# Mixer A's last three row tiles turned by VectorE and DRAM, 1/sum moved into the gate stage, PSUM banks and work order assigned anew

## The chip, the cores and the metric

One core of one Trainium2 chip. The metric is the device time of one execution in microseconds; of the kernel before it is the median of three runs. Instructions run on five engines, each in its own order: TensorE (PE; its weight loads are listed as PEld), VectorE (DVE), ScalarE (ACT), GpSimd (POOL) and SyncE (SP), whose queue issues every DMA of this kernel.

## The reference

One layer of a streaming encoder for a prompt group (1024 rows) and a sample group (32 rows), width 1024, two kinds of attention with 8 heads of 64 each, all in float32:

```python
hn = rmsnorm(h, g_pre)
qa, ka, va, ga, qb, kb, vb, gb = split(hn @ w_in)          # 8 blocks of 512 columns
# A: softmax over the row's own 64-row chunk and the 8 before it, with a clipped relative bias
s = qa @ ka.T * 64 ** -0.5 + bias_table[:, clip(k_pos - q_pos, -128, 128) + 128]
oa = softmax(where(ok, s, -1e30)) @ va
# B: stick breaking, strictly causal
z = qb @ kb.T * 64 ** -0.5
log_1m = where(causal, log_sigmoid(-z), 0)
after = cumsum(log_1m, reverse=True) - log_1m
ob = where(causal, exp(log_sigmoid(z) + after), 0) @ vb
y = concat(oa * silu(ga), ob * silu(gb)) @ w_out
h = h + rmsnorm(y, g_post)
h = h + sigmoid(h @ w_ple_gate) * (p @ w_ple)
```

The outputs are h of both groups and the new keys and values. The sample group attends to cached keys and values beside its own 32.

## The kernel before

**Precision.** Each float32 operand is split into a high part (float32r) and the remainder. A product is then two or three float32r matmuls that accumulate in one PSUM bank. The names ending in `h` and `l`, as `wTh` and `wTl`, are these parts.

**Stages.** First the rows are normalized and turned (`norm_tile`, `turn_x`), while the part `p @ w_ple` of the first four row tiles is computed (`Ple`). Then come eight pairs of heads, in the order A0, B0, A1, B1, A2, B2, A3, B3. While a pair's attention runs, `weave` lays the projections of the next pair (`col_steps`: 24 matmuls of 352 columns for each of 3 column chunks) between its steps. Beside the last pair the eight gate blocks are projected (`gA`, `gB`). Then follow the output projection and the gate of the layer input, each as a block product with seven multiplications for each 2x2 of blocks, whose combined weight blocks (`sum_weights`) are prepared during the attention stages and kept in DRAM.

**Attention of one head** (`attention`). Rows are taken in eight tiles `i` of 128. An A tile reads `cost(i)` key blocks of 128: 1, 2, 3, 4 and then 5 for each of tiles 4 to 7. `scores` multiplies into `S` banks. For A a VectorE operation adds the bias into `w0` (`om`) and keeps the extremum in `m` (`stat`); ScalarE takes the exponential into `w1` (`be`) with the row's sum; VectorE takes the reciprocal of the sum and GpSimd scales `w1` by it. For B there are two sigmoids, a running product on VectorE and a product on GpSimd.

`weights_t` turns the weights, so that keys lie on partitions. On the common path TensorE transposes each 128x128 block into a `T` bank (`ptw`), ScalarE copies up to four blocks to the high part (`wTh`) and VectorE subtracts for the low part (`wTl`). Tiles named in `ROUND` (A: tile 5; B: tiles 4, 5, 6) go another way: VectorE turns 32x32 squares from `w1` to `w0`, one DMA writes them to a DRAM tensor `swap`, four DMAs read them back with the squares in their turned places into `w1`, and the same two engines split the result from there. `values` multiplies the turned weights with V into one `PV` bank for each half of the rows, and the sum of its two halves (`ot`) goes to DRAM (`o_dr`).

**Gates.** A gate chunk (`col_steps`, kind `g`) loads its part of `o_dr` (`og`), takes the sigmoid of its product on ScalarE, multiplies by the product on VectorE and by `og` on GpSimd, and stores to `og_dr`.

**Space.** PSUM has eight banks, shared out by kind: two for projections (`mm`), three for scores (`S`), two for transposes (`T`), one for values (`PV`), each kind taken in turn. In SBUF `w0` and `w1` come out of two rings, `ring0` (`om`, 3076 columns) and `ring1` (`be`, 3640 columns); the other tiles have a tag with a fixed number of buffers.

**Order.** Every operation is recorded with what it must follow. `order` simulates the engines with costs for each operation and emits, whenever an engine is free, the ready operation with the smallest key. The key is a class, then the place in the recording plus a shift from the tables `AHEAD_OF` (by engine and tile name) and `AHEAD_AT` (by stage too). For TensorE the class puts attention (0) ahead of projections (1). All instructions are emitted from line 515, so the profile tells them apart by tile names alone.

Of the kernel before, what the change touches and what calls it, by code (L numbers as in the profile page):

```python
# [28 lines left out]
    ('ACT', 'L'): 329, ('ACT', 'S'): -1196, ('ACT', 'be'): -16, ('ACT', 'kd'): 796,  # L29
    ('ACT', 'newh'): -56, ('ACT', 'oT'): -600, ('ACT', 'om'): -36, ('ACT', 'p'): -23,  # L30
    ('ACT', 'v'): 51, ('DVE', 'Kl'): 1140, ('DVE', 'Vh'): -16, ('DVE', 'gT'): -158,
    ('DVE', 'om'): -178, ('DVE', 'ot'): 166, ('DVE', 'uu'): -34, ('DVE', 'vt'): 131,
    ('DVE', 'wl'): 758, ('DVE', 'wls'): 131, ('POOL', 'kl'): 934, ('POOL', 'wl'): 27,
    ('SP', 'GP'): 272, ('SP', 'Kcs'): -461, ('SP', 'be'): 17, ('SP', 'o'): 49,
    ('SP', 'pp'): -611, ('SP', 'stv'): -823,
}
AHEAD_AT = {
    (0, 'ACT', 'sq'): -249, (0, 'DVE', 'pleo'): -309, (1, 'ACT', 'stv'): 1111, (1, 'DVE', 'stat'): -309,
    (1, 'PE', 'ptw'): 174, (2, 'ACT', 'be'): 54, (2, 'ACT', 'v'): 127, (2, 'ACT', 'wTh'): -885,
    (2, 'ACT', 'wh'): -57, (2, 'DVE', 'S'): -238, (2, 'DVE', 'ot'): -112, (2, 'DVE', 'vx'): -293,  # L40
    (3, 'ACT', 'Kh'): -162, (3, 'ACT', 'be'): 443, (3, 'ACT', 'ot'): -574, (3, 'ACT', 'stq'): 399,
    (3, 'ACT', 'w'): 692, (3, 'ACT', 'wTh'): -1352, (3, 'DVE', 'Kcs'): -84, (3, 'DVE', 'S'): -1167,
    (3, 'DVE', 'Vh'): 222, (3, 'DVE', 'w'): -332, (3, 'PE', 'PV'): 1076, (3, 'PE', 'Ss'): 1432,
    (3, 'SP', 'kd'): -118, (3, 'SP', 'kl'): -63, (4, 'ACT', 'be'): 76, (4, 'ACT', 'om'): 38,
    (4, 'DVE', 'S'): -1067, (4, 'DVE', 'vt'): -1007, (4, 'DVE', 'wTl'): 571, (5, 'ACT', 'stq'): -509,
    (5, 'ACT', 'wh'): 1431, (5, 'DVE', 'stat'): 886, (5, 'DVE', 'vt'): -279, (5, 'POOL', 'om'): -449,
    (6, 'ACT', 'be'): 27, (6, 'ACT', 'v'): 29, (6, 'ACT', 'wTh'): 103, (6, 'DVE', 'om'): 123,
    (6, 'DVE', 'ot'): 37, (6, 'POOL', 'ksS'): 600, (6, 'POOL', 'om'): 364, (6, 'SP', 'be'): 463,
    (7, 'ACT', 'newh'): 1036, (7, 'ACT', 'wTh'): -428, (7, 'DVE', 'L'): -198, (7, 'DVE', 'S'): 1202,
    (7, 'DVE', 'Vl'): -1133, (7, 'DVE', 'kt'): 76, (7, 'DVE', 'om'): 204, (7, 'DVE', 'w'): -825,  # L50
    (7, 'DVE', 'wTl'): -310, (7, 'PE', 'ptw'): 1440, (7, 'SP', 'bias'): -214, (7, 'SP', 'o'): 69,
    (7, 'SP', 'swap'): -328, (8, 'ACT', 'sgg'): -941, (8, 'DVE', 'S'): -79, (8, 'DVE', 'Vl'): 272,
    (8, 'DVE', 'om'): 183, (8, 'DVE', 'sgg'): -911, (8, 'POOL', 'sgg'): 256, (8, 'SP', 'Kcs'): 610,
# [4 lines left out]
}  # L58
# [14 lines left out]

def f(ap):

    return ap.bitcast(F32)

# [443 lines left out]
def stream_step(  # L521
# [945 lines left out]
    for k in range(2):  # L1467
        ple.load_w(k, 0)
# [516 lines left out]
```

## Time and profile before

| | us |
|---|---|
| median of 3 runs (lowest, highest) | 776.47 (776.36, 776.52) |
| the profiled execution | 776.69 |
| its span, first to last instruction | 774.8 |

One profiled execution is read throughout. Rows of grouped instructions give the engine, the operation, the tile written and the tiles read (numbers left out), the shape and the count, then busy time and the mean in ns of one instruction, then the engine's idle time ahead of them with what ended it. Rows in order of time start with the start and the time covered, in us from the span's start. Rows of one tile's instructions give the least, the median and the largest duration in ns, and the first and last start. Rows of DMAs give the count, the KB of each and the median us from issue to landing.

### The profile page before, as it was taken

Reading aid. Unit: us, or ns where it says so; the run is one execution under the profiler, and the core shown is the slowest. Engines: PE = TensorE matmul, PEld = TensorE weight load, DVE = VectorE, ACT = ScalarE, POOL = GpSimd, SP = SyncE. Lnnn points to the kernel's source line nnn. Section 1 sums busy time; section 2 is a strip of 40 time slices with the busy share of each in tenths; the row PEclk is TensorE's granted clock in tenths of the full one; section 3 lists DMA queues with packets and bytes.
Section 4 is the critical chain, followed back from the end, with each engine's and each line's share of the span. In section 5 each row is a group of like instructions: output and inputs, shape, how many; then the busy total and the mean of one; then the engine's idle time right before and its main releaser. Section 6 shows DMA issues by size and latency. Waiting matters only on the chain.

```text
span 774.8 us, 14446 instructions
## 1 busy us (share of the span) xinstructions
PE 764.6 (99%) x4486; PEld 706.7 (91%) x4486; DVE 600.0 (77%) x1127; ACT 526.7 (68%) x1138; POOL 473.1 (61%) x551
## 2 busy tenths in 40 slices
PE   8999999999999999999999999999999999999997
PEld 6999999999999999999999899999998887888786
DVE  6827768788788899777788788778554687998975
ACT  5646775886687777796767786665447878775561
POOL 5626535463686556766877587665652539798533
PEclk9999999999999999999999999999999999999999
DMA  9736645656868748757958877877689957869644
GB/s 298 247 117 183 155 98 163 154 157 179 219 178 236 190 135 254 198 158 237 229 191 223 237 226 207 245 191 221 180 280 297 302 166 227 260 203 343 231 160 136
DMA packets 190303, 161.00 MB, mean 208 GB/s; under 512 B 65346, under 2 KB 155242, under 8 KB 190227
## 3 DMA queue, kind: packets, MB, share of 16 engines
q1 hardware_dynamic: 190226, 160.08, 70.1%
q8 instruction: 36, 0.59, 0.3%
q14 instruction: 41, 0.33, 0.1%
HBM read 98.12 MB, written 53.50 MB: 196 GB/s over the span
## 4 chain that ended last, share of the span: by engine, by line
PE 89%; POOL 3%; DVE 3%; DMA 2%; ACT 1%; issue 1%; SPq 1%; POOLq 0%; ACTq 0%; DVEq 0%
PE mm_vB L515 6%; PE mm_gB L515 6%; PE mm_gA L515 6%; PE mm_qB L515 6%; PE mm_vA L515 5%; PE mm_kB L515 5%; PE mm_kA L515 5%; PE mm_qA L515 4%; PE PVB L515 4%; PE SB L515 4%; PE PVA L515 4%; PE SA L515 4%; PE ptwA L515 3%; PE o3P L515 3%; PE o1P L515 3%; PE g1P L515 3%
## 5 line engine op out<-in xcount | busy, mean ns | idle before, releaser
L515 POOL TENSOR_TENSOR be<-be,om 128x256 f32<-128x256 f32 (+8 forms) x66 | 82.7, 1258 | 72.6 <-DVE om L515 32.0
L515 DVE TENSOR_TENSOR_SCAN om<-om,SB 128x384 f32<-128x384 f32 (+5 forms) x96 | 91.9, 966 | 15.7 <-ACT be L515 8.7
L515 POOL TENSOR_SCALAR be<-be,statA 128x640 f32<-128x640 f32 (+4 forms) x64 | 46.9, 742 | 35.5 <-DVE statA L515 31.7
L515 ACT ACTIVATE om<-SB 128x384 f32<-128x384 f32 (+5 forms) x96 | 46.0, 495 | 20.3 <-DVE SB L515 16.1
L515 ACT ACTIVATE be<-SB 128x384 f32<-128x384 f32 (+5 forms) x96 | 44.7, 497 | 7.8 <-DVE om L515 4.1
L515 ACT ACTIVATE be<-om,statA 128x640 f32<-128x640 f32 (+4 forms) x64 | 44.4, 695 | 6.2 <-DVE statA L515 4.0
L515 DVE TENSOR_TENSOR wTl<-ptwA,wTh 128x512 fp32r<-128x512 f32 (+2 forms) x80 | 37.0, 480 | 12.5 <-ACT wTh L515 11.8
L515 ACT CAST wTh<-ptwA 128x512 fp32r<-128x512 f32 (+2 forms) x80 | 31.8, 427 | 18.2 <-PE ptwA L515 17.6
L515 DVE TENSOR_TENSOR wTl<-be,wTh 128x640 fp32r<-128x640 f32 (+2 forms) x32 | 35.7, 1123 | 6.0 <-ACT wTh L515 5.3
L515 PE MATMUL ptwA<-ident,be 128*128 128x128 f32 x200 | 32.3, 273 | 0.9 <-POOL qsS L515 0.9
L515 PE MATMUL SB<-kdB,LB 128*128 128x384 f32 (+5 forms) x96 | 33.1, 349 | 0.0
L515 PE MATMUL SB<-klB,LB 128*128 128x384 f32 (+5 forms) x96 | 32.7, 345 | 0.0
L515 DVE CUSTOM_DVE_ANT_0 om<-SA,biasA 128x320 f32<-128x320 f32 (+3 forms) x64 | 30.1, 482 | 2.5 <-PE SA L515 2.2
L515 PE MATMUL SA<-kdA,LA 128*128 128x320 f32 (+2 forms) x96 | 30.8, 324 | 0.4 <-DVE statsA L515 0.3
L515 DVE STREAM_TRANSPOSE om<-be 128x640 f32<-128x640 f32 (+2 forms) x32 | 29.8, 932 | 1.1 <-POOL be L515 0.9
L515 PE MATMUL SA<-klA,LA 128*128 128x320 f32 (+2 forms) x96 | 29.6, 314 | 0.0
L515 DVE TENSOR_TENSOR wTl<-ptwB,wTh 128x512 fp32r<-128x512 f32 (+3 forms) x48 | 25.4, 545 | 4.9 <-PE PVB L515 2.4
L515 ACT CAST wTh<-be 128x640 fp32r<-128x640 f32 (+2 forms) x32 | 25.6, 809 | 5.0 <-DMA be<-swapB 4.6
L515 POOL TENSOR_TENSOR klA<-stkA,kdA 64x1024 fp32r<-64x1024 f32 (+2 forms) x9 | 20.0, 2222 | 13.4 <-ACT kdA L515 13.2
L515 ACT CAST wTh<-ptwB 128x512 fp32r<-128x512 f32 (+3 forms) x48 | 22.1, 485 | 8.6 <-PE ptwB L515 5.8
L515 POOL TENSOR_TENSOR gB<-gB,gB 128x256 f32<-128x256 f32 x32 | 26.5, 846 | 2.2 <-DMA kdB<-kdB 1.6
L515 PEld LDWEIGHTS ptwA<-ident,be 128*128 128x128 f32 x200 | 24.8, 140 | 2.6 <-POOL qsS L515 1.2
(696 smaller groups left out, 2653.1 us busy)
## 6 DMA issues: line engine op xcount, KB each, us to landing
oB<-in_w_out_dram SPq DMA_DIRECT2D x16, 256.0 KB, 3.6
sum_dro<-oB SPq DMA_DIRECT2D x16, 256.0 KB, 2.8
gB<-in_w_ple_gate_dram SPq DMA_DIRECT2D x16, 256.0 KB, 4.3
sum_drg<-gB SPq DMA_DIRECT2D x16, 256.0 KB, 2.6
x<-in_x_prompt_dram SPq DMA_DIRECT2D x16, 256.0 KB, 4.0
h_dr<-h SPq DMA_DIRECT2D x8, 512.0 KB, 3.5
ht<-h_dr SPq DMA_DIRECT2D x8, 512.0 KB, 5.7
raw<-sum_drg SPq DMA_DIRECT2D x16, 256.0 KB, 2.9
```

Of the source, the lines that this page charges most:

```text
L515: getattr(getattr(tc.nc, o.what[0]), o.what[1])(*args, **kw)
```

## The change

1. **Tiles.** `ROUND` for A becomes tiles 5, 6 and 7, each by itself, so tiles 6 and 7 of all eight A heads take the path through VectorE and DRAM.
2. **1/sum.** `scores` for A leaves the weights unscaled. The row sums of the 16 tiles of a pair (two heads of eight) are collected in one 128x16 tile; TensorE turns it to 16x128, VectorE takes the reciprocal of the turned tile, and it is stored to DRAM (`over_dr`). Each A gate block loads it, spread over 64 partitions for each head (`over`), and GpSimd multiplies `og` by it ahead of the product with the gate. The sample group's rows have ones there, as their weights are still scaled in place.
3. **PSUM and SBUF.** A bank is given to whichever kind asks, with one or two kept for each kind (`BANKS`). The two rings become one `Heap` of 6880 columns, from which `w0` is taken at the low and `w1` at the high end. The tiles that hold turned keys and values shrink from nine blocks of 128 columns to 1056 columns.
4. **Order.** `order` now simulates once forward by the recording, then computes for each operation backwards from the end the latest time at which it may run (`latest`), and simulates forward again, taking the operation that is due first; the shift tables are all new and are added to the due time, ten ns to the unit. TensorE's operations go by due time too.
5. **The early part of `p @ w_ple`.** Its first 512 input rows are loaded so that a partition holds four neighbouring rows, the result goes to a DRAM tensor in that layout (`ple_early`) and is read back from it; the loads of the second half of `w_ple` are recorded ahead of the first x tiles.
6. **Smaller edits.** The matmuls of one `values` call are chained in their recorded order, its copy waits for the last of them, and constants of the interleaving (`SPACE_S`, `SPACE_T`, `SPACE_V`, `RATES`, `SUMS_STEP`) and of the cost of a GpSimd product differ.

```diff
 AHEAD_OF = {
-    ('ACT', 'L'): 329, ('ACT', 'S'): -1196, ('ACT', 'be'): -16, ('ACT', 'kd'): 796,
...
+    ('ACT', 'L'): -809, ('ACT', 'Qfs'): -495, ('ACT', 'S'): -671, ('ACT', 'be'): 45,
...
-ROUND = {"A": ((5,),), "B": ((4,), (5,), (6,))}
+ROUND = {"A": ((5,), (6,), (7,)), "B": ((4,), (5,), (6,))}
...
-SPACE_S = {'A': 0.15, 'B': 0.05}
-SPACE_T = {'A': 0.35, 'B': 0.4}
-SPACE_V = {'A': 0, 'B': 0}
+SPACE_S = {'A': 0.15, 'B': 0}
+SPACE_T = {'A': 0.35, 'B': 0.35}
+SPACE_V = {'A': 0, 'B': 0.1}
...
-RATES = (1.0, 0.84, 0.92, 0.94, 1.0, 0.88, 1.14, 1.0)
+RATES = (1.0, 0.8, 0.92, 0.94, 1.0, 0.88, 1.02, 1.0)
...
+BANKS = {'mm': 1, 'S': 2, 'T': 1, 'PV': 1}
+PASSES = 1
+PE_LATEST = True
...
-        import heapq
         for place, old in self.turns:
             place.after.update(x[0] for x in old.uses)
...
+        out, end = self.simulate(lambda o: o.key)
+        for n in range(PASSES):
+            self.latest(end)
+            last = n == PASSES - 1
+            out, end = self.simulate(lambda o: (o.key[0], o.index + last * o.shift, o.index) if o.eng == "PE" and not PE_LATEST else (0, o.due + last * 10 * o.shift, o.index))
+        return out
...
+        def grant():
+            while spare:
+                need = sum(max(0, BANKS[k] - held) for k, (b, held) in kinds.items() if b)
+                best = None
+                for k, (b, held) in kinds.items():
+                    if b and b.asked and len(spare) - 1 >= need - (held < BANKS[k]):
+                        x = ranks[min(b.users)]
+                        if best is None or x < best[0]:
+                            best = x, k, b
...
-    ring0, ring1 = Arena(rec, at, "om", 3076), Arena(rec, at, "be", 3640)
+    heap = Heap(rec, at, "be", 6880)
...
+                    if kind == "gA":
+                        over = box["over"] = at2.tile([P, T], F32, tag="stg", name=f"over{p}", bufs=3)
+                        nc.gpsimd.memset(over[:, SEQ:T], 1.0)
+                        for h in range(2):
+                            src = over_dr[p].real[h:h + 1, :].to_broadcast([HD, SEQ])
+                            dma(over[h * HD:(h + 1) * HD, 0:SEQ], Raw(over_dr[p], src))
...
+                if kind == "gA":
+                    nc.gpsimd.tensor_tensor(box["og"], box["og"], box["over"][:, cs], ALU.mult)
                 nc.scalar.activation(sg, acc, AF.Sigmoid)
...
-                nc.scalar.activation(w1[:, 0:n], w0[:, 0:n], AF.Exp, bias=m[:, last:last + 1], scale=-1.0, accum_out=m[:, 3:4])
-                nc.vector.reciprocal(m[:, 3:4], m[:, 3:4])
-                nc.gpsimd.tensor_scalar(w1[:, 0:n], w1[:, 0:n], m[:, 3:4], 1.0, ALU.mult, ALU.mult)
+                if p not in sums:
+                    sums[p] = small.tile([P, 16], F32, tag="rsum", name=f"rsum{p}", bufs=2), []
+                r, seen = sums[p]
+                r = r[:, 8 * h + i:8 * h + i + 1]
+                nc.scalar.activation(w1[:, 0:n], w0[:, 0:n], AF.Exp, bias=m[:, last:last + 1], scale=-1.0, accum_out=r)
+                seen.append(i)
+                if len(seen) == 16:
+                    over = psum("T", f"ptr{p}")[0:16, 0:P]
+                    nc.tensor.transpose(over, sums[p][0], ident)
+                    r = at.tile([P, 2 * P], F32, tag="ot", name=f"over{p}", bufs=3)[0:16, 0:P]
+                    nc.vector.reciprocal(r, over)
+                    dma(over_dr[p].rearrange("h (t q) -> (h t) q", q=P), r)
             state[i] = w0, w1
...
                 nc.tensor.matmul(acc[:, c], v2[:, b, :], w, start=(n == 0), stop=(n == len(todo) - 1))
+                if n:
+                    rec.ops[-1].after.add(rec.ops[-2])
...
-                src = src.rearrange("(b p) c -> p b c", p=P)
+                src = src.rearrange("(p b) c -> p b c", b=4)
...
-    SUMS_STEP = {2: [10, 31], 4: [10, 22], 5: [3, 30], 6: [8, 28]}
+    SUMS_STEP = {2: [10, 31], 4: [10, 26], 5: [7, 30], 6: [8, 28]}
...
     ple.load_p(0, 2)
     for k in range(2):
         ple.load_w(k, 0)
+    for k in range(2):
+        ple.load_w(k, 1)
     xs = {0: load_x(0)}
     xs[1] = load_x(1)
-    for k in range(2):
-        ple.load_w(k, 1)
     xs[2] = load_x(2)
```

More of the change, by code (lines that the diff above doesn't have):

```diff
@@ L36 @@
+    ('POOL', 'om'): 197, ('POOL', 'rs'): -497, ('POOL', 's'): -1046, ('POOL', 'sgg'): 929,
[4 rows of a table added]
 }
 AHEAD_AT = {
[L38 to L41, printed above, removed]
@@ L48 @@
[L48 to L53, printed above, removed]
[4 rows of a table removed]
+    (0, 'ACT', 'pleo'): 1195, (0, 'ACT', 'sq'): 1380, (0, 'ACT', 'stk'): -1095, (0, 'ACT', 'v'): 1160,
@@ L206 @@
 class Op:
-    __slots__ = ("pieces", "eng", "what", "args", "kw", "key", "busy", "late", "ready", "left", "after", "at", "size", "shared", "table")
+    __slots__ = ("pieces", "eng", "what", "args", "kw", "key", "busy", "late", "ready", "left", "after", "at", "size", "shared", "table", "start", "shift", "due", "size_", "index", "users", "tiles", "old")
 LAND = {"PE": 165, "ACT": 0, "DVE": 0, "POOL": 0, "SP": 0, "CTL": 0}
@@ new lines, in simulate, with leave @@
+        for n, b in first.items():
+            b.asked = self.ops[n].left == 1
+        grant()
+        for heap in self.heaps:
+            heap.clear()
+            heap.grant(come)
+        def leave(b):
+            if b.line is False:
+                spare.append((b.gone, b.bank, b))
+                kinds[b.tag][1] -= 1
+                grant()
+                return
+            if b.line is None:
+                b.heap.give(b)
+                b.heap.grant(come)
+                return
+            new = nexts[b.line]
+            if new is not None:
+                nexts[b.line] = new.next
+                new.room, new.place.old = b.room, (b,)
+                come(new.place, b.gone)
```

323 lines of the change are left out of this document (257 added, 66 removed), and 33 rows, old and new, of tables (AHEAD_AT, AHEAD_OF).

## The prediction

> **What bounds the kernel now.** I read the page's busy times first, then the chain that ended last, then the stretches in which mixer A's attention runs.
>
> ```profile
> span 774.8 us, 14446 instructions
> PE 764.6 (99%) x4486; PEld 706.7 (91%) x4486; DVE 600.0 (77%) x1127; ACT 526.7 (68%) x1138; POOL 473.1 (61%) x551
> PE 89%; POOL 3%; DVE 3%; DMA 2%; ACT 1%; issue 1%; SPq 1%; POOLq 0%; ACTq 0%; DVEq 0%
> q1 hardware_dynamic: 190226, 160.08, 70.1%
> ```
>
> TensorE is busy in 764.6 of 774.8 us and carries 89% of the chain; the next engine, VectorE, stands at 77%. So work taken off TensorE shortens the run unless what replaces it comes late. The second table has one row for each stretch with A's scores (pairs A0 to A3) and one for the last B pair with the A gates. The columns are the stretch, its length, then busy us and instructions of PE, PEld, DVE, ACT and POOL, the clock, the DMA share and GB/s.
>
> ```profile
> 62.00:106.00 44.00, 44.00 (x295) 43.27 (x294) 32.18 (x99) 32.21 (x76) 24.85 (x35) 1.00 0.62 155
> 164.00:216.00 52.00, 52.00 (x343) 50.64 (x342) 43.36 (x115) 37.52 (x88) 29.33 (x39) 1.00 0.73 199
> 289.00:330.00 41.00, 40.95 (x265) 39.52 (x264) 35.33 (x94) 30.72 (x71) 28.21 (x31) 1.00 0.83 229
> 400.00:450.00 50.00, 48.56 (x311) 45.84 (x310) 42.11 (x109) 38.37 (x88) 35.96 (x45) 1.00 0.87 239
> 450.00:546.00 96.00, 96.00 (x615) 93.72 (x615) 78.82 (x138) 60.82 (x136) 65.54 (x72) 1.00 0.77 219
> ```
>
> TensorE stands full even there, at full clock; visible gaps in the four A rows are 0.05 and 1.44 us. VectorE is at 73 to 86%, and DMA is fullest in the last two.
>
> **Term 1: transposes taken off TensorE.** Row tiles 6 and 7 of each A head have five key blocks each (tile 5 goes through VectorE already). Eight heads times ten is 80 of the 200 `ptwA` transposes. Their price is read from starts, since a matmul's shown length overlaps the next.
>
> ```profile
> 186.65 1.45 PE L515 MATMUL mm_kB<-hnh,wh_kB 128*128 128x352 f32 x8
> 187.94 0.60 PE L515 MATMUL ptwA<-ident,be 128*128 128x128 f32 x4
> 188.29 1.21 PE L515 MATMUL mm_kB<-hnh,wl_kB 128*128 128x352 f32 x6
> 189.34 0.27 PE L515 MATMUL ptwA<-ident,be 128*128 128x128 f32 x1
> L515 PE MATMUL ptwA<-ident,be 128*128 128x128 f32 x200 | 32.3, 273 | 0.9 <-POOL qsS L515 0.9
> ```
>
> Eight projection matmuls take 187.94 - 186.65 = 1.29 us, 0.161 each. From 186.65 to 189.34 (2.69 us) fourteen of them and four transposes start: 2.69 - 14 x 0.161 = 0.43, or 0.108 each. The upper end is the group's 32.3 us by 200, 0.16 each. I take 0.108, as the matmuls around them would close up: 80 x 0.108 = 8.6 us off (12.9 at the upper end). Four transposes of the 16-column sums come in, one for each pair, at 0.108 at most: 0.4 us back. Net -8.2 us.
>
> **Term 2: what the other engines do instead.**
>
> ```profile
> L515 DVE TENSOR_TENSOR wTl<-ptwA,wTh 128x512 fp32r<-128x512 f32 x32 | 21.5, 679 | 9.3 <-ACT wTh L515 9.0
> L515 DVE TENSOR_TENSOR wTl<-ptwA,wTh 128x128 fp32r<-128x128 f32 x32 | 8.9, 279 | 1.4 <-ACT wTh L515 1.2
> L515 DVE TENSOR_TENSOR wTl<-be,wTh 128x640 fp32r<-128x640 f32 x16 | 17.2, 1075 | 2.5 <-ACT wTh L515 2.0 <-DMA kdA<-kdA 0.3
> L515 DVE STREAM_TRANSPOSE om<-be 128x640 f32<-128x640 f32 x16 | 13.3, 832 | 0.3 <-POOL be L515 0.2
> L515 DVE RECIPROCAL statA<-statA 128x1 f32<-128x1 f32 x64 | 9.2, 155 | 6.1 <-ACT be L515 5.6
> L515 POOL TENSOR_SCALAR be<-be,statA 128x640 f32<-128x640 f32 (+4 forms) x64 | 46.9, 742 | 35.5 <-DVE statA L515 31.7
> L515 POOL TENSOR_TENSOR sggA<-sggA,oggA 128x352 f32<-128x352 f32 x12 | 13.7, 1146 | 4.2 <-DMA oggA<-o_dr 2.5 <-DVE sggA L515 1.7
> L515 ACT CAST wTh<-be 128x640 fp32r<-128x640 f32 (+2 forms) x32 | 25.6, 809 | 5.0 <-DMA be<-swapB 4.6
> ```
>
> A tile on the old path cost VectorE 0.679 + 0.279 = 0.958 us; on the new path it costs 0.832 + 1.075 = 1.907. An A pair has four such tiles, +3.8 us, and loses 16 reciprocals of 0.144 (9.2 by 64), -2.3: +1.5 us of VectorE per A pair, 6.0 in all, beside a full TensorE. In 289 to 330 that makes 36.8 us in a stretch that wants to shrink from 41 to 38.8 (a fourth of 8.6 less). It fits, with 2 us to spare; without that cover each pair costs its 1.5. ScalarE keeps its casts. It is the one that waits for the swap to land: 4.6 us over 32 casts now, so about 2.3 more for 16, while evictions and exponentials queue behind it; at 68% it bears that.
>
> GpSimd loses 64 scalings (46.9 us) and gets 12 multiplications of the gate's kind, 12 x 1.146 = 13.8 us, all beside the A gates: 65.5 + 13.8 = 79 of 96 us. The gated product is read back only for the output projection, so lateness there has until the B gates end. Besides, each score tile's way to its transpose loses two links, 0.155 and 0.742 us.
>
> The Trainium skill bears on the VectorE price, "SBUF — State Buffer", section "Who interferes with whom": a VectorE instruction with two SBUF inputs contends with a GpSimd instruction that reads SBUF, one blocking the other. The next rows agree in kind, and by that rule 64 fewer GpSimd instructions would make the 1.075 nearer the row's least, 0.798, 0.28 x 16 = 4.4 us less of VectorE; the sum does not use it.
>
> ```profile
> L515 DVE TENSOR_TENSOR wTl<-ptwA,wTh x80: 251/473/693, 72.1 to 467.9; 128x128 fp32r<-128x128 f32 x32, 128x512 fp32r<-128x512 f32 x32, 128x256 fp32r<-128x256 f32 x8, 128x384 fp32r<-128x384 f32 x8
> L515 DVE TENSOR_TENSOR wTl<-be,wTh x32: 798/1011/1842, 86.4 to 547.9; 128x640 fp32r<-128x640 f32 x16, 128x768 fp32r<-128x768 f32 x8, 128x896 fp32r<-128x896 f32 x8
> ```
>
> **Term 3: DMA and its queue.** Each tile writes 320 KB to DRAM and reads it back in four parts; 16 tiles make 16 + 64 issues, and the sums 4 + 8 more.
>
> ```profile
> swapA<-om SPq DMA_DIRECT2D x8, 320.0 KB, 3.5
> be<-swapA SPq DMA_DIRECT2D x32, 80.0 KB, 2.5
> L515 SPq DMA_DIRECT2D be<-swapA x32: 357/452/1351, 77.9 to 462.8; - x32
> 400.14 0.34 SPq L515 DMA_DIRECT2D swapB<-om  x1
> 448.62 1.08 SPq L515 DMA_DIRECT2D out_dram<-ktB  x2
> ```
>
> The 74 issues from 400.14 to 448.62 take 40.9 us, summed over the queue's timeline rows of that stretch (the first and the last are shown). Twenty more at 0.452 are 9.0 us: 49.9 in a stretch of 50 that should shrink to 47.8. Bytes rise by 4 x 640 KB, 2.6 MB by 50 us or 52 GB/s on 239. So the queue has no room left in the last two A stretches, but in the others and in the B stretches between them it has, and outputs and weight sums can slip there. I cost it at nothing; the price without that cover is the slow rival's.
>
> **Term 4: order, PSUM banks, head and tail.** All order is new, and no row shows it. Below, the gain is nothing. Above, it is all of TensorE's late starts: against the median interval of each matmul shape, the starts from the first to the last row below (4486 on the page) run late by 26.9 us, 6.9 of that before 60 us. Of the other 20.0, 6.5 stand ahead of a matmul of A's chain (scores 3.2, values 1.7, transposes 1.6). I take 2.7, two fifths of 6.5, as 80 of the 200 transposes and both removed links are A's.
>
> ```profile
> 1.30 2.93 PE L515 MATMUL idle<-newh 128*128 128x256 f32 x12 [1.30 <-DVE newh L515]
> 3.00 0.91 SPq L515 DMA_DIRECT2D om<-in_x_prompt_dram  x2
> 3.95 1.07 SPq L515 DMA_DIRECT2D wpr_1True<-in_w_ple_dram  x2
> 12.88 0.66 PE L515 MATMUL ptx<-ident,be 128*128 128x128 f32 x4 [1.22 <-DVE be L515]
> 769.59 0.29 PE L515 MATMUL g3P3b<-gB,wlS4g 128*128 128x256 f32 x1
> ```
>
> At the head two weight loads are recorded ahead of the first x tiles: if issued so, x starts 1.07 us later and the transposes at 12.88 wait for it; the early inputs, now contiguous per partition, give some of it back. I take nought, with 1.1 either way. The closing of the run after 769.59 is not touched.
>
> **Sum.** 774.8 - 8.2 - 2.7 = 763.9 us of span. The profiled execution took 776.69, 1.9 outside its span, and lies 0.2 above the median of 776.47: 763.9 + 1.9 - 0.2 = **765.6 us**.
>
> **The rivals.** *More from the order* (0.12): half of the 20.0 us goes, 776.5 - 8.2 - 10 = 758. For it: any kind of tile may take any bank. Against: TensorE shows only some 2 us of gaps between 20 and 767.
>
> *VectorE becomes late in A's stretches* (0.13): it idles 5.7 of 41 us in 289 to 330; if those waits stay, the stretch needs 36.8 + 5.7 = 42.5 against 38.8, +3.7. With one such stretch in full, 776.5 - 8.2 + 3.7 = 772. By the Trainium skill, "VectorE: DVE Perf Modes", section "Rules for kernel authors", a 128x128 transpose belongs on TensorE where a PSUM destination will do; that speaks for this rival.
>
> *The gain doesn't come through* (0.06): two such stretches, 776.5 - 8.2 + 7.4 = 775.7, as good as no change.
>
> *SyncE's queue decides* (0.13), slower: it issues in order, and 9.1 of its 50 us in the last A stretch are waits for producers. If these stay, the 9.0 us of new issues come on top; in the last two A stretches 18.0, so 776.5 - 8.2 + 18 = 786. It decides from 8.2 us on, that is from a little under half of that. Against it: issues can be pulled ahead of such waits.
>
> *The forecast* (0.56): 762 to 769.
>
> **How the numbers follow.** Faster is 0.56 + 0.12 + 0.13 = 0.81, same 0.06, slower 0.13, where 0.2%, 1.6 us, is what a measurement can tell. The range from 758 to 776 leaves out the slow rival and the lower half of the best case.
>
> **What would show it.** `ptwA` down from 200 to 120 and four small transposes; TensorE's busy time near 754, still 99%; `be` scalings by `statA` gone from GpSimd; STREAM_TRANSPOSE of 128x640 from 16 to 32. VectorE near 606. Wrong would be: gaps of TensorE above 4 us between 60 and 460 behind `wTh` or `wTl` (VectorE, SyncE), or a late first `mm_kA` (head).

## The result and the profile after

| | before | changed |
|---|---|---|
| median of 6 runs (lowest, highest), us | 776.30 (775.69, 776.52) | 773.10 (770.49, 774.36) |
| the profiled execution, us | 776.69 | 773.43 |
| its span, us | 774.8 | 771.7 |

The ratio is 0.9957, with a 95% interval of 0.9941 to 0.9974: faster by 0.43%, 3.2 us where 10.9 were forecast. The runs of the changed kernel spread over 3.9 us, those of the kernel before over 0.8.

The first lines of the page, of the chain and of the queue, for the changed kernel:

```profile
span 771.7 us, 14284 instructions
PE 758.4 (98%) x4410; PEld 698.9 (91%) x4410; DVE 611.6 (79%) x1067; ACT 525.0 (68%) x1122; POOL 447.2 (58%) x503
PE 86%; DVE 4%; DMA 4%; SPq 3%; issue 1%; ACT 1%; DVEq 0%; POOL 0%; ACTq 0%; POOLq 0%
q1 hardware_dynamic: 202258, 172.70, 77.1%
```

TensorE lost 6.2 us of busy time, the span only 3.1. The chain now runs through VectorE, the DMAs and SyncE's queue for 11% of the span together; before it was 6%. VectorE gained 11.6 us instead of 6.0. The groups of instructions that the change touches, shapes kept apart (busy us and mean ns behind the first bar, the engine's idle time ahead of them behind the second):

```profile
L780 PE MATMUL ptwA<-ident,be 128*128 128x128 f32 x120 | 21.4, 273 | 1.3 <-DVE statA L780 1.3
L780 DVE TENSOR_TENSOR wTl<-ptwA,wTh 128x512 fp32r<-128x512 f32 x16 | 10.7, 675 | 0.7 <-PE PVA L780 0.5 <-ACT wTh L780 0.3
L780 DVE TENSOR_TENSOR wTl<-ptwA,wTh 128x128 fp32r<-128x128 f32 x16 | 4.4, 274 | 3.5 <-ACT wTh L780 2.3 <-PE PVA L780 1.1
L780 DVE TENSOR_TENSOR wTl<-be,wTh 128x640 fp32r<-128x640 f32 x32 | 32.1, 1008 | 9.2 <-ACT wTh L780 6.4 <-DMA be<-swapB 2.5 <-DMA gB<-in_w_ple_gate_dram 0.3
L780 DVE STREAM_TRANSPOSE be<-be 128x640 f32<-128x640 f32 x32 | 26.2, 827 | 0.5 <-ACT be L780 0.3
L780 DVE RECIPROCAL over<-ptr 16x128 f32<-16x128 f32 x4 | 3.8, 946 | 2.5 <-DMA o_dr<-otA 1.6 <-DMA o_dr<-diagsA 0.8
L780 ACT CAST wTh<-be 128x640 fp32r<-128x640 f32 x32 | 23.3, 729 | 7.3 <-DMA be<-swapA 5.6 <-DMA be<-swapB 1.4
L780 POOL TENSOR_TENSOR oggA<-oggA,over 128x352 f32<-128x352 f32 x12 | 12.6, 1047 | 4.7 <-DMA oggA<-o_dr 4.0 <-DVE Kl1sB L780 0.8
```

The counts are those of the change: 120 `ptwA`, 32 turnings of 128x640, 12 multiplications by `over`. On VectorE the low parts from `be` rose from 17.2 to 32.1 us, the turnings from 13.3 to 26.2, the low parts from `ptwA` fell from 30.4 (two shapes) to 15.1 and the reciprocals from 9.2 to 3.8: together 14.9 + 12.9 - 15.3 - 5.4 = 7.1 us. The other 4.5 us of the 11.6 are in operations that the change doesn't touch.

The same stretches as before, with the three B stretches between them added (106 to 164, 216 to 289 and 330 to 400); first the changed kernel, then those three of the kernel before:

```profile
62.00:106.00 44.00, 44.00 (x289) 43.37 (x289) 34.18 (x79) 31.31 (x67) 15.18 (x19) 1.00 0.75 201
106.00:164.00 58.00, 57.88 (x359) 55.77 (x359) 49.24 (x79) 44.45 (x99) 33.30 (x36) 1.00 0.62 173
164.00:216.00 52.00, 52.00 (x342) 50.70 (x341) 42.31 (x101) 39.33 (x88) 17.38 (x22) 1.00 0.75 198
216.00:289.00 73.00, 70.72 (x441) 67.06 (x440) 63.63 (x106) 51.54 (x118) 50.37 (x60) 1.00 0.77 206
289.00:330.00 41.00, 40.78 (x261) 38.25 (x259) 35.33 (x86) 31.92 (x72) 16.97 (x20) 1.00 0.86 244
330.00:400.00 70.00, 68.22 (x423) 65.73 (x422) 58.62 (x84) 51.58 (x107) 50.27 (x60) 1.00 0.86 239
400.00:450.00 50.00, 47.65 (x309) 45.36 (x308) 39.09 (x99) 36.03 (x84) 25.82 (x31) 1.00 0.94 243
450.00:546.00 96.00, 96.00 (x610) 93.91 (x609) 80.45 (x125) 59.90 (x131) 72.63 (x83) 1.00 0.86 240
```

```profile
106.00:164.00 58.00, 58.00 (x363) 56.45 (x363) 47.10 (x72) 43.11 (x94) 28.14 (x36) 1.00 0.47 132
216.00:289.00 73.00, 73.00 (x470) 70.70 (x469) 63.83 (x110) 54.49 (x124) 46.84 (x57) 1.00 0.65 185
330.00:400.00 70.00, 69.68 (x440) 67.29 (x439) 54.50 (x90) 51.05 (x115) 50.12 (x65) 1.00 0.70 193
```

TensorE now shows gaps of 2.28, 1.78 and 2.35 us in three stretches (216 to 289, 330 to 400, 400 to 450) where there were 0, 0.32 and 1.44, and the first two are B's. DMA rose by 12 and 16 points in these two. VectorE's added time stands in B's stretches too: it was busy in 171.5 us of the three, 165.4 before, and in 150.9 us of A's four, 153.0 before. What TensorE waited for longest between 60 and 460 us (us in all, times, longest):

```profile
PE ptwA L780 <- DVE statA L780: 1.3, 1, 1.3
PE SsB L780 <- DVE QlsB L780: 1.1, 1, 1.1
PE ptwB L780 <- ACT be L780: 1.0, 2, 0.7
PE ptwB L780 <- ACT stvB L780: 0.9, 1, 0.9
```

Two of these waits in order of time (start, time covered):

```profile
343.49 0.73 ACT L780 CAST wTh<-be 128x640 fp32r<-128x640 f32 x1 [1.95 <-DMA be<-swapA]
344.13 0.45 ACT L780 COPY stvB<-mm_vB 128x352 f32<-128x352 f32 x1
344.72 0.30 PE L780 MATMUL ptwB<-ident,be 128*128 128x128 f32 x1 [0.87 <-ACT stvB L780]
```

```profile
259.07 2.37 POOL L780 TENSOR_TENSOR klA<-stkA,kdA 64x1024 fp32r<-64x1024 f32 x1 [0.31 <-ACT kdA L780]
259.19 2.54 DVE L780 TENSOR_TENSOR QlsB<-QfsB,QhsB 128x256 fp32r<-128x256 f32 x1
261.78 0.39 PE L780 MATMUL SsB<-Kh0sB,QlsB 128*128 128x272 f32 x1 [1.10 <-DVE QlsB L780]
```

In the first, ScalarE stands at an A tile's swap that has not landed; the eviction behind it is late, and a B transpose waits for that. So lateness of A's round trip shows up in B, on TensorE. In the second, a VectorE product takes 2.54 us beside one of GpSimd, and a matmul of B's scores waits for it.

**Where the gain went.** Visible gaps are a small part of lateness, so I use the bookkeeping of the prediction again: each matmul shape, transposes apart, is given its median interval from start to start. The sum of these medians is called the work; what single intervals exceed the median by, where that is over 25 ns, is called late starts. Intervals below the median, or just above it, make up the rest.

| us | before | changed | difference |
|---|---|---|---|
| work | 748.5 | 740.6 | -7.9 |
| late starts | 26.9 | 34.2 | +7.3 |
| the rest | -7.1 | -9.7 | -2.6 |
| first to last matmul start | 768.3 | 765.1 | -3.2 |

The work fell as forecast. It is counts at medians, so it tells what was taken off and not that the run got shorter by it; how the shapes are grouped, and whose medians are taken, moves work and rest against each other by 1 us or a little more. Late starts rose by nearly as much, by any of these counts: from 19.3 to 27.2 us between 62 and 546 us, while those of the head fell from 6.9 to 5.8. B's three stretches have 6.4 us of that rise (6.7 to 13.1) and A's four 2.2 (10.2 to 12.4); ahead of `ptwB` alone they rose from 0.4 to 5.0. The question for the experiments is what brings them.

### The profile page after: what moved, and what is told of

Read it like the earlier page. It is cut to its first block, busy times and chain, and to the rows that moved or that the text cites. A ratio compares the mean times of both kernels' runs of the same rounds, so it can differ in the third digit from the quotient of the medians.

```text
span 771.7 us, 14284 instructions
## 1 busy us (share of the span) xinstructions
PE 758.4 (98%) x4410; PEld 698.9 (91%) x4410; DVE 611.6 (79%) x1067; ACT 525.0 (68%) x1122; POOL 447.2 (58%) x503
## 4 chain that ended last, share of the span: by engine, by line
PE 86%; DVE 4%; DMA 4%; SPq 3%; issue 1%; ACT 1%; DVEq 0%; POOL 0%; ACTq 0%; POOLq 0%
PE mm_gA L780 6%; PE mm_gB L780 6%; PE mm_kA L780 6%; PE mm_qA L780 5%; PE mm_kB L780 5%; PE mm_vA L780 5%; PE mm_qB L780 4%; PE PVB L780 4%; PE mm_vB L780 4%; PE SB L780 4%; PE PVA L780 3%; PE ple L780 3%; PE SA L780 3%; SPq L780 3%; PE g0P L780 3%; PE g2P L780 3%
## 5 line engine op out<-in xcount | busy, mean ns | idle before, releaser
L780 POOL TENSOR_TENSOR be<-be 128x128 f32<-128x128 f32 (+8 forms) x66 | 85.1, 1294 | 48.6 <-DVE be L780 23.0
L780 DVE TENSOR_TENSOR_SCAN be<-be,SB 128x384 f32<-128x384 f32 (+5 forms) x96 | 91.5, 963 | 8.2 <-ACT be L780 4.3
L780 ACT ACTIVATE be<-SB 128x384 f32<-128x384 f32 (+4 forms) x192 | 83.4, 497 | 18.2 <-DVE be L780 7.0
L780 ACT ACTIVATE be<-be,statA 128x640 f32<-128x640 f32 (+3 forms) x64 | 44.5, 696 | 11.6 <-DVE statA L780 11.5
L780 DVE STREAM_TRANSPOSE be<-be 128x640 f32<-128x640 f32 (+3 forms) x56 | 47.9, 866 | 3.4 <-POOL be L780 2.3
L780 DVE CUSTOM_DVE_ANT_0 be<-SA,biasA 128x320 f32<-128x320 f32 (+3 forms) x64 | 29.7, 481 | 4.4 <-PE SA L780 3.4
L780 POOL TENSOR_TENSOR gB<-gB,gB 128x256 f32<-128x256 f32 x32 | 26.9, 861 | 9.8 <-DMA gB<-in_w_ple_gate_dram 7.9
L780 POOL TENSOR_TENSOR oB<-oB,oB 128x256 f32<-128x256 f32 x32 | 25.6, 826 | 6.7 <-DMA oB<-in_w_out_dram 4.8
L780 PE MATMUL ptwB<-ident,be 128*128 128x128 f32 x144 | 26.5, 274 | 2.4 <-ACT be L780 1.0
L780 POOL TENSOR_TENSOR klB<-stkB,kdB 64x1024 fp32r<-64x1024 f32 x8 | 20.0, 2504 | 14.0 <-ACT kdB L780 12.1
L780 POOL TENSOR_TENSOR klA<-stkA,kdA 64x1024 fp32r<-64x1024 f32 (+2 forms) x9 | 19.3, 2150 | 14.4 <-ACT kdA L780 9.5
L780 DVE TENSOR_TENSOR wTl<-ptwA,wTh 128x128 fp32r<-128x128 f32 (+3 forms) x48 | 21.8, 478 | 5.3 <-ACT wTh L780 3.5
L780 POOL TENSOR_TENSOR wl_vB<-wr_vB,wh_vB 128x512 fp32r<-128x512 f32 x8 | 10.5, 1309 | 24.5 <-DMA stvA<-swapA 13.3
```

Source lines behind the costliest of these rows:

```text
L780: getattr(getattr(tc.nc, o.what[0]), o.what[1])(*args, **kw)
```

## The experiments

**The theories.** T1, the order: taking the tiles off TensorE gives its 8 us, and the new order with its banks brings the late starts. T2, the path: the load of the new path (VectorE, SyncE's queue, DRAM) brings them. T3, the fit: the shift tables fit the work they stand beside and nothing else, so a kernel with one of the two exchanged is slower for that alone. T4, the queue: among T2's loads it is SyncE's queue that decides. The first two were stated first, T3 after the first four runs, and T4 under its name only when the price of added issues was known. All ratios are against runs of the kernel before, taken beside them on the same chip; its medians there were 776.15 to 777.03. Late starts are those of one profiled execution of each kernel. Intervals at a lowered clock count among them: the last section works out what that is in `b_tiles`.

### The work and the order exchanged

`b_tiles` is the kernel before with the three tiles on the new path; `b_both` has the late division by the sums too (with `ring1` 32 columns shorter, to make room).

```diff
-ROUND = {"A": ((5,),), "B": ((4,), (5,), (6,))}
+ROUND = {"A": ((5,), (6,), (7,)), "B": ((4,), (5,), (6,))}
```

> The kernel before with the tiles alone: A's tiles 6 and 7 go through VectorE and DRAM, weights are still scaled in place, and order, banks and rings stay as before. Theory 1 (the new order and its banks bring the late starts, the tiles give their 8 us wherever they are): 768 to 769. Theory 2 (the path through VectorE, the DMA queue and DRAM itself brings late starts that eat most of it): 773 or more.

> The kernel before with the tiles and the deferred 1/sum, order, banks and rings as before (the ring of w1 is 32 columns shorter to make room for the sums). Theory 1: 768 or a little under, as GpSimd's scalings leave the way to the transposes too. Theory 2: 773 or more, near the changed kernel's 773.1.

`a_tile5` is the changed kernel with that line turned back; `a_order` also scales the weights in place, as before, and so is the new order with the old work.

```diff
-ROUND = {"A": ((5,), (6,), (7,)), "B": ((4,), (5,), (6,))}
+ROUND = {"A": ((5,),), "B": ((4,), (5,), (6,))}
...
-                nc.scalar.activation(w1[:, 0:n], w0[:, 0:n], AF.Exp, bias=m[:, last:last + 1], scale=-1.0, accum_out=r)
...
+                nc.scalar.activation(w1[:, 0:n], w0[:, 0:n], AF.Exp, bias=m[:, last:last + 1], scale=-1.0, accum_out=m[:, 3:4])
+                nc.vector.reciprocal(m[:, 3:4], m[:, 3:4])
+                nc.gpsimd.tensor_scalar(w1[:, 0:n], w1[:, 0:n], m[:, 3:4], 1.0, ALU.mult, ALU.mult)
```

> The changed kernel with A's tiles 6 and 7 back on TensorE, 1/sum still in the gate stage. Theory 1: 781, as the 80 transposes come back at 0.108 us each. Theory 2: 774 to 777: TensorE's work grows by 8.6 us, and the late starts fall by some 5.

> The changed kernel with A's tiles 6 and 7 back on TensorE and the weights scaled in place: the new order, banks, heap and early inputs alone. Theory 1: 8 us above the changed kernel, 781. Theory 2: near the kernel before, 774 to 777, since the late starts go with the tiles.

| | median us | ratio (95%) | late starts us |
|---|---|---|---|
| `b_tiles` | 828.41 | 1.0653 (1.0628, 1.0678) | 82.0 |
| `b_both` | 831.78 | 1.0686 (1.0657, 1.0716) | 80.3 |
| `a_tile5` | 791.47 | 1.0174 (1.0147, 1.0201) | 46.1 |
| `a_order` | 788.47 | 1.0137 (1.0114, 1.0159) | 42.1 |

All four lose, and `a_tile5` and `a_order` by more than either theory had expected. The old order, with its rings and banks, can't carry the new path (+52 us). TensorE's longest waits in `b_tiles`:

```profile
PE SA L515 <- DVE statA L515: 7.3, 3, 4.6
PE SB L515 <- ACT be L515: 5.8, 4, 3.1
PE mm_kB L515 <- ACT stkB L515: 5.0, 1, 5.0
PE SB L515 <- DVE om L515: 4.2, 4, 2.1
```

They stand behind the two engines that split the turned weights. But `a_order` has the old work and loses as well, so any exchange loses, and the four don't tell T1 from T2. That suggested T3, and the next step is to take the tables out.

### The same without shift tables

```diff
-AHEAD_OF = {
...
+AHEAD_OF = {}
+AHEAD_AT = {}
```

Five kernels: `b_plain` and `bb_plain` in the old order with the old and the new work, `ao_plain` and `a_plain` in the new order with the old and the new work, and `at_plain`, run later, in the new order with the tiles but the weights scaled in place.

> The kernel before with both shift tables empty. Theory 3: 785 to 810, as its tables fitted it too. Theory 1: within 5 us of 776.

> The kernel before with the tiles and the deferred 1/sum, tables empty, rings, banks by kind and one forward pass as before. Theory 3: about 8 us below the kernel before with empty tables, if the old space and order carry the tiles at all. Theory 2, or too little room in the old rings: well above it, as with the tables (831.8).

> The same with A's tiles 6 and 7 on TensorE and the weights scaled in place, tables empty. Theory 3: the removal of work can be read here without the tables' fit: about 8 us above the run with tiles and sums moved. Theory 2 (the path through VectorE, the queue and DRAM brings late starts of its own): equal to that run or below it.

> The changed kernel with both shift tables empty, so that its two passes alone give the order. Theory 3 (the fit of the shift tables to this very work sets how late TensorE starts): 785 to 800, with late starts of 15 us and more above the changed kernel's 34. Theory 1 (the passes and free banks make the order, well or badly): within 5 us of 773.

> The changed kernel with both tables empty and the weights scaled in place: the tiles without the deferred 1/sum. Between 778.8 (neither) and 779.4 (both) if each part gives and takes nothing. If the tiles alone bring the late starts and the sums give some back, 781 to 785; if the sums bring them (gate stage, the wide reciprocal), 771 to 775.

| | median us | ratio (95%) | work us | late starts us | VectorE us |
|---|---|---|---|---|---|
| `b_plain` | 800.53 | 1.0299 (1.0274, 1.0323) | 751.3 | 49.2 | |
| `bb_plain` | 831.95 | 1.0725 (1.0680, 1.0770) | 741.3 | 87.0 | |
| `ao_plain` | 778.80 | 1.0020 (1.0005, 1.0034) | 747.6 | 29.2 | 610.4 |
| `at_plain` | 777.35 | 1.0004 (0.9993, 1.0014) | 738.9 | 36.1 | 616.1 |
| `a_plain` | 779.35 | 1.0032 (1.0013, 1.0050) | 740.7 | 36.7 | 620.0 |

The page's first row of `ao_plain` and of `at_plain`:

```profile
PE 764.8 (99%) x4486; PEld 708.8 (91%) x4486; DVE 610.4 (79%) x1127; ACT 527.1 (68%) x1138; POOL 481.2 (62%) x551
PE 757.5 (98%) x4406; PEld 699.3 (90%) x4406; DVE 616.1 (80%) x1127; ACT 524.7 (68%) x1122; POOL 489.3 (63%) x551
```

In the new order without tables, computed anew for each kernel by the same rules, the tiles take 8.7 us of work off and bring 6.9 us of late starts; the late division on top changes nothing for the better (+2.0 us; `at_plain` lies between the ranges expected). So the new work as a whole is worth -1.5 us with the tiles alone, at the edge of what these intervals can tell, and +0.5 with both, within it. That speaks against T1: the new order with the old work has 29.2 us of late starts, near the 26.9 of the tuned kernel before, and the lateness comes with the path. What the shared banks add under the new work, no run separates. TensorE's longest waits in `at_plain`:

```profile
PE PVA L713 <- DVE wTl L713: 2.4, 1, 2.4
PE PVA L713 <- ACT wTh L713: 1.6, 2, 0.9
PE ptwB L713 <- ACT be L713: 1.6, 1, 1.6
```

The first two stand behind the two operations that split the weights come back from DRAM. The new order, with its banks, its heap and its early part of `p @ w_ple`, is worth 800.5 - 778.8 = 21.7 us for the old work when neither is tuned. Its tables then take 779.35 to 773.1, -6.2; the old tables took 800.5 to 776.7, -24. In other work the new tables cost instead: `ao_plain` against `a_order` 9.7. That bears T3 out, but not in the size expected, as `a_plain` without tables was to reach 785 or more. And T3 doesn't explain the losses of the new work in the old order: `bb_plain`, without tables, is as slow as `b_both` with them (831.95 and 831.78). Whether there the path itself loses or the room in the old rings, no run tells apart.

### Load added to the changed kernel, unplanned

These hooks sit where the instructions are issued, so that the order is the changed kernel's, row for row, with one load added at each of the 16 turnings of tiles 6 and 7. `a_xdve` adds three VectorE products of 128x128, `a_xissue` five DMAs of 512 bytes, `a_xbytes` one DMA of 640 KB (within DRAM). `a_group67` turns tiles 6 and 7 in one DMA round trip: 40 issues fewer.

```diff
+                    if o.what == ("vector", "transpose") and o.args[0].buf.name[:3] == "omA" and o.args[0].buf.name[-2:] in ("_6", "_7"):
+                        for _ in range(3):
+                            m = self.extra.get()
+                            tc.nc.vector.tensor_tensor(m, m, m, ALU.max)
```

```diff
+                        for _ in range(5):
+                            tc.nc.sync.dma_start(self.extra[0][self.extra[2]], self.extra[1])
+                            self.extra[2] += 1
...
+    rec.extra = [dram.tile([80, 128], F32, tag="extra", name="extra"), w_in[0, 0, 0:128], 0]
```

```diff
+                        tc.nc.sync.dma_start(self.extra[0][self.extra[2]], self.extra[1])
+                        self.extra[2] += 1
...
+    rec.extra = [dram.tile([16, 160, 1024], F32, tag="extra", name="extra"), w_gate[0, 0:160, :], 0]
```

```diff
-ROUND = {"A": ((5,), (6,), (7,)), "B": ((4,), (5,), (6,))}
+ROUND = {"A": ((5,), (6, 7)), "B": ((4,), (5,), (6,))}
```

> The changed kernel in its own order, with three more VectorE products of 128x128 (they write the mask onto itself) behind each 32x32 turning of A's tiles 6 and 7: 16 times about 0.9 us, as much VectorE time as the tiles' new path costs net. If the late starts come from VectorE's load, the time rises by about 5 us (to 778); if VectorE's load is covered, by under 1.5.

> The changed kernel in its own order, with five more DMAs of 512 bytes, DRAM to DRAM, issued at each of these 16 places: 80 more issues, as many as the tiles brought, and hardly a byte. If the late starts come from the queue's issue time, plus 5 us or more; if issues are covered, under 1.5.

> The changed kernel in its own order, with one more DMA of 640 KB, DRAM to DRAM, at each of these 16 places: the bytes that the tiles brought once more, for one issue each. If the late starts come from the DMA engines' load, plus 5 us or more; if it is covered, under 1.5.

> The changed kernel with tiles 6 and 7 of a head in one round trip of 1280 columns in place of two of 640: 40 issues fewer, the same bytes and VectorE work, and the order is computed anew, tables kept. If issue time decides, 770 or less; if not, 773 to 790, as the tables no longer fit and a round trip is longer.

| | median us | ratio (95%) | over the changed kernel | late starts us |
|---|---|---|---|---|
| `a_xdve` | 784.71 | 1.0102 (1.0084, 1.0120) | +11.6 | 45.8 |
| `a_xissue` | 809.16 | 1.0413 (1.0394, 1.0433) | +36.1 | 69.3 |
| `a_xbytes` | 796.57 | 1.0246 (1.0219, 1.0274) | +23.5 | 57.0 |
| `a_group67` | 791.03 | 1.0192 (1.0172, 1.0212) | +17.9 | 48.9 |

The added rows of `a_xdve`, `a_xissue` and `a_xbytes` (least, median, largest ns):

```profile
L784 DVE TENSOR_TENSOR maskb<-maskb x48: 240/292/2431, 73.1 to 464.2; 128x128 f32<-128x128 f32 x48
```

```profile
L783 SPq DMA_DIRECT2D extra<-in_w_in_dram x80: 489/587/1727, 74.3 to 485.9; - x80
```

```profile
L782 SPq DMA_DIRECT2D extra<-in_w_ple_gate_dram x16: 517/532/1499, 72.3 to 471.8; - x16
```

VectorE's busy time rose by 18.4 us and the run by 11.6; 80 issues of 0.587 us are 47 us and cost 36; 16 issues with 10 MB cost 23.5, 1.5 us for each DMA, though each takes the queue only about 0.53 us. Some of each price is clock: the mean granted clock of the profiled executions was 0.996, 0.982 and 0.987, against 1.000 for the changed kernel, which at these lengths is an estimated 3, 15 and 10 us. In an order fixed beforehand each kind of load comes through at a good part of its price. `a_group67` would have been the relief by T4; its tables don't fit it (T3), and it says nothing of the queue.

### Was the queue as tight before, and can it be relieved?

`b_xissue` puts the 80 issues into the kernel before, behind the last transpose of tiles 6 and 7. `a_actq` and `b_actq` let ScalarE issue the stores of the new keys and values (SyncE's issues 970 to 866, and 878 to 774).

```diff
+                    if o.what == ("tensor", "transpose") and o.args[0].buf.name[:4] == "ptwA" and o.args[0].buf.name[-4:] in ("_6_4", "_7_4"):
+                        for _ in range(5):
+                            tc.nc.sync.dma_start(self.extra[0][self.extra[2]], self.extra[1])
+                            self.extra[2] += 1
```

```diff
+        rec.ops[-1].what = ("scalar", "dma_start")
```

> The kernel before in its own order, with five more DMAs of 512 bytes, DRAM to DRAM, behind the last transpose of each A tile 6 and 7: the same 80 issues as in the changed kernel's run with more issues (plus 36 us there). If the change used up the room in SyncE's queue, the kernel before has that room: plus 15 us or less. If the queue was as tight before, plus 30 or more.

> The changed kernel in its own order, with the stores of new keys and values issued by ScalarE and not by SyncE, at the same places of the order. If SyncE's queue makes the late starts (theory 4), 767 to 770, late starts back near 27 us. If it doesn't, 772 to 776, as ScalarE pays for the issues.

> The same stores issued by ScalarE in the kernel before. Theory 4, the change having used up the room in the queue: 775 to 778, nothing gained, as there was room. If the queue was as tight before: 770 to 773.

| | median us | ratio (95%) | against the kernel without the edit |
|---|---|---|---|
| `b_xissue` | 805.80 | 1.0363 (1.0341, 1.0385) | +29.2 |
| `a_actq` | 783.15 | 1.0074 (1.0049, 1.0099) | +10.1 |
| `b_actq` | 787.67 | 1.0135 (1.0116, 1.0155) | +11.1 |

The longest waits of TensorE and of ScalarE for a DMA in `b_xissue`:

```profile
PE PVA L515 <- ACT wTh L515: 10.6, 4, 4.3
```

```profile
ACT wTh L515 <- DMA be<-swapA: 16.1, 6, 5.5
```

The queue had nearly as little room before: +29 against +36. So a full queue was not made by the change, and the round trips of tile 5 alone suffice for the chain queue, swap, ScalarE, TensorE. Handing stores to ScalarE lost both times, against every value expected; that its own order was filled by the plan too is the likely reason, but not shown. The two runs don't show that the queue doesn't bind, since they put the load on another engine.

### Load added where the plan sees it

`ao_plain`, the old work in the new order, is given one part of the new path at tiles 6 and 7, recorded, so that the order is computed with it: `aop_dve` one VectorE product of 128x640 ahead of the transposes, `aop_dma` the round trip (one write, four reads; 80 issues, 10 MB in all).

```diff
+            if ab == "A" and i > 5:
+                nc.vector.tensor_tensor(w1[:, 0:n * P], w1[:, 0:n * P], w1[:, 0:n * P], ALU.max)
```

```diff
+            if ab == "A" and i > 5:
+                dr = scratch([P, n * P], f"swap{nm}_{i}")
+                dma(dr, w1[:, 0:n * P])
+                for c in range(4):
+                    x = dr[32 * c:32 * c + 32].rearrange("k (g x) -> k g x", g=4)
+                    dma(w1[32 * c:32 * c + 32, 0:n * P].rearrange("k (g x) -> k g x", g=4), x)
```

> The new order with empty tables, A's tiles 6 and 7 on TensorE and scaled in place (778.8 by itself), with one more VectorE operation on each such tile's 640 columns ahead of its transposes (the larger of the weights and themselves), which the planner knows of: about 1 us each, the net VectorE time that the new path costs. TensorE saves nothing here. If VectorE's time is what eats the 8 us saved: 783 to 787. If not: 778 to 781.

> The same kernel with a round trip of each such tile's weights through DRAM ahead of its transposes, unchanged in value: one write and four reads, 80 issues and the bytes and the delay of the new path, known to the planner. TensorE saves nothing. If the round trip (queue, bytes, delay) is what eats the 8 us: 784 to 788. If not: 778 to 781.

| | median us | ratio (95%) | over `ao_plain` | late starts us |
|---|---|---|---|---|
| `aop_dve` | 792.63 | 1.0208 (1.0186, 1.0230) | +13.8 | 43.6 |
| `aop_dma` | 783.71 | 1.0087 (1.0065, 1.0109) | +4.9 | 36.6 |

The added row of `aop_dve`, then TensorE's longest wait in it:

```profile
L713 DVE TENSOR_TENSOR be<-be 128x640 f32<-128x640 f32 x16 | 16.1, 1009 | 0.1
```

```profile
PE PVB L713 <- ACT wTh L713: 4.4, 3, 2.4
```

Here the two loads part. Eighty issues, and their bytes on top, cost 4.9 us if the order knows of them and 36 (without the bytes) if it doesn't. VectorE's time is not absorbed by knowing: 16.1 us cost 13.8 (5.6 us above the range expected), 0.86 of it, against 0.63 of it unplanned. That speaks against T4 where the order is computed with the issues in it: there the queue gives way more than VectorE does.

The two prices are rough, for four reasons. Each compares one untuned order with another, and how far such orders differ by chance was not measured. The mean granted clock of the profiled execution was 0.994 in `ao_plain`, 0.995 in `aop_dve` and 0.999 in `aop_dma`; 0.005 of 780 us is 3.9, so at one clock the round trip would cost some 9 us, as an estimate. VectorE's busy time is no fixed sum: the page of `aop_dma` has 13 us less of it than that of `ao_plain`, for the same 1127 instructions, and yet it is the slower.

```profile
PE 766.4 (98%) x4486; PEld 706.5 (90%) x4486; DVE 597.2 (76%) x1127; ACT 524.1 (67%) x1138; POOL 480.2 (61%) x551
```

And neither run has the real path's saving on ScalarE's and VectorE's old operations. That the added product stands in the chain from score to transpose explains little of its price: the round trip stands there too and takes longer (1.0 us for the product; medians of 3.5 and 2.5 us from issue to landing for the write and the reads).

As an estimate from these two prices: `at_plain` has 5.7 us more of VectorE than `ao_plain`, 4.9 us by 0.86, and the round trip at 4.9; against 8.7 saved that is +1.1, where -1.5 was measured. The two payments are of the size of the saving. Which of them pays how much stays open.

## Why the prediction was right in sign and wrong in size

**Term 1 held.** -8.2 us was forecast; the work fell by 7.9 between the two kernels and by 8.7 for the tiles alone in the new order without tables. Counts were as forecast. TensorE's busy time, forecast near 754, fell only to 758.4: lateness too short to show as a gap counts as busy. The intervals between starts tell it, the busy time doesn't.

**Term 2 failed, at "It fits, with 2 us to spare".** VectorE's price was near: 7.1 us in the touched groups against 6.0. The error within it is the 16x128 reciprocal, 0.946 us and 3.8 in all, for which no term stood; the 32 low parts, at 1.008 us instead of the 1.075 taken, gave 2.1 of it back. So the Trainium skill's rule on SBUF inputs, named in the prediction, which would have allowed 0.28 less for each, showed as 0.07, with 25.9 us less of GpSimd's busy time (473.1 to 447.2; -33.1 was forecast). The failing step is the next one: time put on VectorE was taken as free as long as the sum stayed below the stretch. In `aop_dve`, 16.1 us of it cost 13.8. Nor did it stay in A's stretches: VectorE's 35.33 us in 289 to 330 did not become 36.8, and its added time, and most of the added late starts, stand in B's. So a sum below the stretch is not cover: an engine must be there at the moment a bank or a tile is wanted. That VectorE, rather than the round trip, brought B's late starts is not shown. The Trainium skill's rule that I held against the change ("VectorE: DVE Perf Modes", "Rules for kernel authors": a 128x128 transpose goes to TensorE where PSUM will do) points to the measured side: without tables the move is worth 1.5 us of the 8.7.

**Term 3 failed, at "I cost it at nothing".** In the new order without tables the round trip alone costs 4.9 us, or some 9 at one clock. The slow rival's price, 18 us, was as wrong: SyncE's queue was feared as a sum of issue times, and an order that knows the issues finds places for them. Unplanned, in the very orders of both kernels, they do cost that: 36 and 29 us for 80.

**Term 4 was wrong in sign as a term.** I took 2.7 us of the late starts as going away with the removed links of A's chain; those ahead of A's scores, values and transposes fell by 0.5 and the whole grew by 7.3. The bound below, "the gain is nothing", was not a bound, since the parts costed at nothing put their lateness here. As to the order itself, with its banks and its heap, it does much more than the term allowed, -21.7 us for the old work, but against an untuned order; against the tuned one before it is +2.1 (`ao_plain`, 1.0020), and only its own tables, -6.2, bring the new kernel under.

**The head** was rightly left at nought. The first x transposes came later by 1.78 us, and the first `mm_kA` by 1.0:

```profile
14.66 0.60 PE L780 MATMUL ptx<-ident,be 128*128 128x128 f32 x4
L780 PE MATMUL mm_kA<-hnh,wh_kA x96: 317/323/415, 20.9 to 363.6; 128*128 128x352 f32 x96
```

The latter started at 19.9 before. As late starts ahead of 60 us fell by 1.1, TensorE had other work to do meanwhile.

**The rivals.** The measured 773.1 lies between *VectorE becomes late* (772) and *the gain doesn't come through* (775.7), which had 0.19 together; their mechanism, lateness that eats the saving, is the one that the runs bear out, except that I looked for it on VectorE and in A's stretches only. It came mostly in B's, ahead of `ptwB`; in 330 to 400 VectorE rose from 54.50 to 58.62 us. The sign named in the prediction came true in its size: TensorE's waits between 60 and 460 us come to some 6 us, over the 4 named, but they stand behind `statA`, `QlsB`, `be` and `stvB`, not behind `wTh` or `wTl`. So the sign of the change came right by luck rather than by the sum: the forecast of 762 to 769 rested on covers that were not there, and the tables' fit, which no term held, decided it.

**What the 3.2 us are.** From the runs: new order without tables against the tuned kernel before, +2.1; new work in it, +0.5; its tables, -6.2. The sum is -3.6, measured -3.2. Split in this way, the speedup is what the fit of the tables brought. It doesn't follow that the moved transposes brought nothing under these tables: tables fitted to the old work in the new order were not tried, and might do as well, better or worse. No kernel of these runs is faster than the changed one.

## What to carry to other kernels

Where the other engines stand at 60 to 80% beside a full one, and the order is planned in detail, price moved work by what it adds to the other engines too, and call nothing hidden because sums fit in a stretch. Judge a change of work and a change of order apart, with the tuning taken out of both: in a tuned kernel every single edit lost (10 to 55 us here), whatever it was worth in an order of its own. On an engine that shows 99%, count late starts from the intervals between starts, since the busy time hides them.

## What the runs showed of the hardware

**The granted clock fell in stretches where TensorE waited.** Two stretches of `b_tiles`:

```profile
216.00:289.00 73.00, 59.81 (x341) 55.67 (x340) 57.31 (x100) 47.51 (x105) 35.63 (x50) 0.90 0.65 178
450.00:600.00 150.00, 135.12 (x798) 126.54 (x797) 115.67 (x228) 89.27 (x203) 89.95 (x106) 0.92 0.74 206
```

Its clock was 0.90 and 0.92 there, with single waits up to 3.1 and 4.6 us, against 1.00 in the same stretches of both kernels. A stretch of `a_plain`, with the one wait that TensorE shows in it:

```profile
62.00:106.00 44.00, 42.10 (x264) 40.91 (x263) 31.80 (x75) 27.80 (x63) 12.34 (x16) 0.96 0.69 184
```

```profile
PE PVA L713 <- DVE wTl L713: 1.9, 1, 1.9
```

The Trainium skill ("TensorE: Matmul & The Clock Gate", Part 1) has the clock halved after some 3.4 us of idleness. The halving agrees, as `b_tiles` shows a clock of 0.50 from 280.7 to 290.8 us; the length doesn't, as the clock of `a_plain` fell with one wait of 1.9 us. A wait therefore costs more than itself. The mean clock of `b_tiles` was 0.970 over its 825.6 us, against 0.999 in the kernel before: by 0.029 of that time, as an estimate, 24 of its 52 us are this.

**The turned reciprocal costs as much as six of the sixteen that it replaces.** 16x128, with 128 elements in a partition, took 946 ns, and 128x1 in the kernel before 155 ns (by the mean of a row).

**One product took six times its usual time beside GpSimd.**

```profile
L515 DVE TENSOR_TENSOR QlsB<-QfsB,QhsB 128x256 fp32r<-128x256 f32 x2 | 0.8, 408 | 0.0
```

`QlsB` of 128x256 averages 408 ns in the kernel before (the row above) and took 2.54 us beside the 2.37 us of `klA`. This agrees with the Trainium skill's rule on two SBUF inputs ("SBUF — State Buffer", "Who interferes with whom"), named in the prediction; so does the largest of the 48 products of `a_xdve`, 2431 ns beside a median of 292:

```profile
330.48 2.39 POOL L780 TENSOR_TENSOR klB<-stkB,kdB 64x1024 fp32r<-64x1024 f32 x1 [1.52 <-DMA klB<-klB]
330.59 3.99 DVE L784 TENSOR_TENSOR maskb<-maskb 128x128 f32<-128x128 f32 x3
```

The three products together take 3.99 us here, the first of them 2.43, and GpSimd's one beside them 2.39. In both cases a short product that started just behind a long one of GpSimd ended within 0.3 us after it.
